# Attention probabilities of four head pairs per layer, turned by transposing DMA transfers instead of TensorE

## The chip, the cores and the metric

The kernel runs on one core of a Trainium2 chip. The metric is the device time of one execution in microseconds (us). The five engines of the core run their own instruction streams and wait for each other by semaphores: TensorE (PE; PEld is its weight load), VectorE (DVE), ScalarE (ACT), GpSimd (POOL) and SyncE (SP). SP, ACT and POOL also issue DMA transfers, each from a queue of its own (SPq, ACTq, POOLq).

## What is computed

Two decoder layers on 256 tokens of width 2048. Each layer has a mixer and a SwiGLU network. In the mixer one input projection feeds two groups of heads: eight heads of sparse attention (DSA: an indexer picks the 64 best keys of a query) and eight heads of latent attention (MLA). The part that matters here is, per head,

```
logits = einsum('bthd,bshd->bhts', q, k) * scale
p = softmax(where(mask, logits, -inf))
out = einsum('bhts,bshd->bthd', p, v)
...
mix = einsum('bse,ed->bsd', concatenate([out_a, out_b]), w_o)
```

All in float32. The sparse group is computed as a masked one, with a bias that is very negative where a key was not picked.

## The kernel before

A matrix is streamed from HBM in units of 512 KB (256 rows by 512 columns), one unit per `load_unit`. SP loads a unit into a raw buffer (line 342, a ring of four, `RAW`). ScalarE writes the high word of its values (`wh`, line 429) and VectorE the rest (`wl`, line 430), into a ring of five (`UNITS`). TensorE then runs 12 matmuls of 512 columns per unit (high by high, high by low, low by high, for two halves of the rows and two token tiles; lines 393 to 395). After each unit `tick()` advances side tasks, which are Python generators: a task that says `yield n` goes on n units later. So the code says after which unit a step is written; a scheduler then sets each engine's own order by the times that it reckons with, and a step may move past rows of other steps on that engine.

The attention of a pair of heads is such a task, `attend`. Logits of both heads go into PSUM (`att`; lines 800 and 804 for MLA, 835 for DSA), VectorE scales and masks them into tiles `lg` (one for the first 128 queries with 128 keys, one for the second with 256), ScalarE takes the exponentials, VectorE normalises. Three units later TensorE turns the probabilities, six 128 by 128 transposes per pair (`transpose4`, line 426), ScalarE copies them out of PSUM (`pr`, line 585), and a unit later TensorE multiplies by the values (lines 592 and 593) and ScalarE and VectorE split the result into `oA` or `oB`.

A layer has four MLA pairs (M0 to M3) and four DSA pairs (D0 to D3), and the units around them belong to other projections. From about 200 us on (layer 0) they come in this order: key block KA1 (8 units), query block QA1 (8 units), value block VA1 (8 units), then w_o. D0 and D1 run beside KA1, M2 and M3 beside QA1, D2 and D3 beside VA1.

One side task already turns tiles by DMA: `heads_T` (for QA0, KA1 and QA1) evacuates a projection to `hd`, ScalarE copies its 32-bit words apart into a plane of low and one of high halfwords (`pl`, line 630), its own queue issues a transposing transfer (line 633), and ScalarE interleaves the halves again (`qk`, line 639). The hidden layer does the same from SP's queue (lines 1068, 1074 and 1079). Tiles `lg`, `pl`, `pr`, `hd` and the work tiles of the rotation (`ra`, `rb`) share two rings of four and six buffers (`t2`), so a new one waits for the last reader of the old.

In the background GpSimd loads, stores and VectorE adds "pre-sums" (`presums`, tiles `q`, lines 853 to 873) for the network behind, paced by the splits.

Of the kernel before, what the change touches and what calls it, by code (L numbers as in the profile page):

```python
# [27 lines left out]
U16 = mybir.dt.uint16  # L28
AF = mybir.ActivationFunctionType
# [4 lines left out]
P = 128  # L34
D = 2048
S = 256
NT = S // P
# [27 lines left out]
SOON = 200  # L65
FIRSTD = 2
LAND = 5
BEHIND_D, LANDH = 2, 9
T2, T2MORE = 4, 6
ALLFROM, SETSFROM, EARLY = 3, 4, 0  # L70
# [17 lines left out]
def hybrid_trunk(ctx: ExitStack, tc: tile.TileContext, x, xt_in, pos, w_in, g_cq, g_ckv, w_uq,  # L88
                 w_ukv, w_o, ln1_g, ln1_b, ln1_T, w_gu, w_down, ln2_g, ln2_b, ln2_T, out):
    nc = tc.nc  # L90
# [7 lines left out]
    def nm(s):  # L98
        uid[0] += 1
        return f"{s}{uid[0]}"  # L100

    def t8(shape, dt, s):
        return sb.tile(shape, dt, name=nm(s), tag="a8", bufs=10)
# [13 lines left out]
    def pt(shape, dt, s, tag=None, bufs=1):  # L117
        assert phase["name"] == "att"
        return phase["pool"].tile(shape, dt, name=nm(s), tag=tag or s, bufs=bufs)
# [4 lines left out]
    def t2(shape, s, dt=F32):  # L124
        if phase["name"] == "att":
            phase["t2"] = phase.get("t2", 0) + 1
            if phase["t2"] * T2MORE % (T2 + T2MORE) < T2MORE:
                return pt(shape, dt, s, "t2", T2MORE)
        return sb.tile(shape, dt, name=nm(s), tag="t2", bufs=T2)
# [10 lines left out]
    def in_turn(s, first, n):  # L140
        turns[s] = turns.get(s, -1) + 1
        return bank(first + turns[s] % n, s)
# [4 lines left out]
    def trp():  # L147
        return in_turn("tr", 4, 2)

    def att():  # L150

        return ps.tile([P, 2, C], F32, name=nm("att"), tag="b67", bufs=1)
# [58 lines left out]
    def causal(m, t):  # L211
        return m if t else m[:, P:]
# [98 lines left out]
    def spawn(gen):  # L311
        task = [0, gen]
        tasks.append(task)
        step(task)
        return task

    def behind(*before):
        while any(b in tasks for b in before):
            yield 1
# [33 lines left out]
    latest = {}  # L353
# [70 lines left out]
    def transpose4(srcs, psum):  # L424
        for i, s in enumerate(srcs):
            nc.tensor.transpose(psum[:, i * P:(i + 1) * P], s, ident)

    def split(hi, lo, src):
        high = nc.scalar.activation(hi, src, AF.Copy)  # L429
        nc.vector.tensor_tensor(lo, src, f(hi), op=ALU.subtract)  # L430
        return high.ins
# [123 lines left out]
    def softmax_head(lg, t, n):  # L555

        mx = small([P, 1], "mx")
        nc.vector.tensor_reduce(mx, lg, axis=AX.X, op=ALU.max, negate=True)
        sm = small([P, 1], "sm")
        nc.scalar.activation(lg, lg, AF.Exp, bias=mx, accum_out=sm)  # L560
        rc = small([P, 1], "rc")
        nc.vector.reciprocal(rc, sm)
        nc.vector.tensor_scalar(lg, lg, rc, None, ALU.mult)

    def attend(logits_of, scale, bias, v_of, oh, ol, h0, wait=3):


        lgs = []
        lp = att()
        logits_of(h0, [[lp[:, j, 0:P], lp[:, j, P:3 * P]] for j in range(2)])  # L570
        for t in range(NT):
            n = P * (t + 1)
            lg = t2([P, 2, n], "lg")
            nc.vector.scalar_tensor_tensor(lg, lp[:, :, t * P:t * P + n], scale,
                                           bias[t].unsqueeze(1).to_broadcast([P, 2, n]), op0=ALU.mult, op1=ALU.add)
            for j in range(2):
                softmax_head(lg[:, j, :], t, n)
            lgs.append(lg)
        yield wait
        prs = []  # L580
        for j in range(2):
            tp = trp()
            transpose4([lgs[0][:, j, :], lgs[1][:, j, 0:P], lgs[1][:, j, P:]], tp)
            pr = t2([P, 3 * P], "pr")
            nc.scalar.activation(pr, tp[:, :3 * P], AF.Copy)
            prs.append(pr)
        yield 1
        op = trp()
        for j, pr in enumerate(prs):
            v0, v1 = v_of(h0 + j)  # L590
            ov = op[:, j * S:(j + 1) * S]
            mm(ov, v0, pr[:, 0:S], start=True, stop=False)
            mm(ov[:, P:], v1, pr[:, S:], start=False, stop=True)
        split(oh.rearrange("p j t -> p (j t)"), ol.rearrange("p j t -> p (j t)"), op)


    def layer(l, xT, norms, last):
# [10 lines left out]
        def heads_T(o, nh, hd, rot, cos, sin, dst, soon=False):  # L608
# [18 lines left out]
            for s in ss:  # L627
# [7 lines left out]
                yield 1  # L635
            yield LAND
            for t in range(NT):
# [134 lines left out]
        oT = {}  # L772
# [12 lines left out]
        def mla_attend(hp, m, wait, *before):  # L785

            yield wait
            yield from behind(*before)
            qn, kn, vb = m
            if "B" not in oT:  # L790
                oT["B"] = [t8([P, M_HEADS, S], F32R, "oB") for _ in range(2)]

            def logits(h0, dst):


                ts = [slice(t * P, (t + 1) * P) for t in range(NT)]
                for j in range(2):
                    for t in range(NT):
                        h = (h0 + j) % 4
                        mm(dst[j][t], qn[:, h, ts[t]], kn[:, h, :P * (t + 1)], start=t == 0, stop=False)  # L800
                for t in range(NT):
                    for j in range(2):
                        pr = slice(64 * j, 64 * j + 64)
                        mm(dst[j][t], qpT[pr, h0 // 2, ts[t]], kpT[pr, :P * (t + 1)], start=False, stop=t == NT - 1)

            h0 = 2 * hp
            yield from attend(logits, M_SCALE, [causal(masks["c"], t) for t in range(NT)],
                              lambda h: (vb[:, 0, (h % 4) * P:(h % 4 + 1) * P], vb[:, 1, (h % 4) * P:(h % 4 + 1) * P]),
                              oT["B"][0][:, h0:h0 + 2, :], oT["B"][1][:, h0:h0 + 2, :], h0, 3 if hp else 4)

        def dsa_qk(b, soon=False):
            dst = t4([P, 4, S], F32, "qk")
# [11 lines left out]
        def dsa_attend(hp, kaT, qaT, va, wait, *before):  # L824

            yield wait
            yield from behind(*before)
            if "A" not in oT:
                oT["A"] = [t8([P, A_HEADS, S], F32R, "oA") for _ in range(2)]

            def logits(h0, dst):
                for j in range(2):
                    for t in range(NT):
                        h = (h0 + j) % 4
                        mm(dst[j][t], qaT[:, h, t * P:(t + 1) * P], kaT[:, h, :P * (t + 1)], start=t == 0,
                           stop=t == NT - 1)

            h0 = 2 * hp
            yield from attend(logits, A_SCALE, bias,
                              lambda h: (va[:, 0, (h % 4) * P:(h % 4 + 1) * P], va[:, 1, (h % 4) * P:(h % 4 + 1) * P]),  # L840
                              oT["A"][0][:, h0:h0 + 2, :], oT["A"][1][:, h0:h0 + 2, :], h0)

        ready = {}

# [57 lines left out]
        bias = [pt([P, P * (t + 1)], F32, f"selb{t}") for t in range(NT)]  # L902
# [10 lines left out]
        if l == 0:  # L913
# [6 lines left out]
                             [sinM[:, t] for t in range(NT)], qpT, True))  # L920
        m = mla_half(0)
        b = [spawn(mla_attend(0, m, 1, p_qp)), spawn(mla_attend(1, m, 4, p_qp))]
        qa, p_qa = dsa_qk(QA0)
        va = dsa_v(VA0)
        finish(*b)
        a = [spawn(dsa_attend(i, ka, qa, va, 3 + 3 * i, p_ix, p_ka, p_qa)) for i in range(2)]
        m = mla_half(1)
        ka, p_ka = dsa_qk(KA1)
        b = [spawn(mla_attend(2 + i, m, 1 + 3 * i)) for i in range(2)]
        qa, p_qa = dsa_qk(QA1)  # L930
        va = dsa_v(VA1)
        finish(*a, *b)
        a = [spawn(dsa_attend(2 + i, ka, qa, va, 1 + 3 * i, p_ka, p_qa)) for i in range(2)]


# [424 lines left out]
```

## Time and profile before

| | us |
|---|---|
| median of 3 runs | 2131.24 |
| lowest, highest | 2130.05, 2131.3 |
| profiled execution | 2130.67 |
| its span (first to last instruction) | 2128.9 |
| TensorE busy in the span | 2114.6 |
| VectorE, ScalarE, GpSimd busy | 1855.1, 1363.7, 326.8 |

The granted TensorE clock was 0.998. In rows of groups, the number after the bar is the busy time of all, the next the mean of one in ns; in rows of instructions the three numbers are minimum, median and maximum in ns. In rows of waits stand the sum in us, how often, and the longest. In rows of the chain stand start and length in us. Rows of windows give, after the window, its length and each engine's busy time, then TensorE's granted clock, the share of time that the DMA engines were busy, and GB/s.

### The profile page before, as it was taken

How to read it: one execution, taken by the hardware profiler on the slowest of the kernel's cores; microseconds unless marked ns; L12 is line 12 of the kernel's file. 1: busy time of each engine (PE TensorE's matmuls, PEld its weight loads, DVE VectorE, ACT ScalarE, POOL GpSimd, SP SyncE). 2: the span in 40 equal slices, each digit the busy share in tenths (PEclk: the TensorE clock that was granted, in tenths of full speed). 3: DMA queues.
4: the chain of work that ended last, by engine and by line, in shares of the span. 5: the costliest groups of instructions: out<-in, count | busy, mean ns of one | idle time of the engine just before them, and what ended most of it. 6: DMA issues, size and time to landing. Idle time of an engine off the chain costs nothing.

```text
span 2128.9 us, 28292 instructions
## 1 busy us (share of the span) xinstructions
PE 2114.6 (99%) x9836; PEld 1754.3 (82%) x9836; DVE 1855.1 (87%) x2346; ACT 1363.7 (64%) x1735; POOL 326.8 (15%) x523
## 2 busy tenths in 40 slices
PE   9999999999999999999999999999999999999998
PEld 8888888888888888888888888888888888888886
DVE  7696776899999999999867976678999999999997
ACT  6556654766666667776655556457667676777773
POOL 1222220021111110110012232201111111110111
PEclk9999999999999999999999999999999999999999
DMA  8688888588889999998657888885989998999994
GB/s 312 205 298 294 309 297 312 183 229 258 242 256 278 290 295 293 279 266 265 217 178 240 302 290 293 319 287 187 249 260 252 286 276 272 296 283 292 293 304 118
DMA packets 191903, 567.11 MB, mean 266 GB/s; under 512 B 47776, under 2 KB 48080, under 8 KB 191120
## 3 DMA queue, kind: packets, MB, share of 16 engines
q1 hardware_dynamic: 127776, 403.10, 53.8%
q0 software_dynamic: 51024, 158.67, 29.1%
q10 hardware_dynamic: 12960, 3.54, 1.0%
q8 instruction: 77, 1.26, 0.2%
q14 instruction: 66, 0.54, 0.1%
HBM read 504.94 MB, written 31.46 MB: 252 GB/s over the span
## 4 chain that ended last, share of the span: by engine, by line
PE 85%; DVE 8%; issue 3%; DMA 2%; ACT 2%; SPq 0%; POOL 0%; DVEq 0%; ACTq 0%; POOLq 0%
PE acc L393 9%; PE acc L395 9%; PE acc L394 9%; PE acc L1222 7%; PE acc L1223 7%; PE acc L1221 7%; PE gu_p L1106 5%; PE gu_p L1107 5%; PE gu_p L1104 5%; DVE wl L430 4%; PE gu_c L1106 3%; PE gu_c L1107 3%; PE gu_c L1104 3%; PE att L1106 2%; PE att L1107 2%
## 5 line engine op out<-in xcount | busy, mean ns | idle before, releaser
L429 ACT ACTIVATE wh<-raw 128x1024 fp32r<-128x1024 f32 (+2 forms) x923 | 944.4, 1050 | 518.1 <-PE acc L395 125.8
L430 DVE TENSOR_TENSOR wl<-raw,wh 128x1024 fp32r<-128x1024 f32 (+2 forms) x923 | 1088.0, 1212 | 189.0 <-ACT wh L429 187.0
L393 PE MATMUL acc<-wh,xhl 128*128 128x512 f32 (+1 forms) x756 | 297.0, 394 | 0.0
L395 PE MATMUL acc<-wh,xhl 128*128 128x512 f32 (+1 forms) x756 | 292.1, 387 | 0.0
L394 PE MATMUL acc<-wl,xhl 128*128 128x512 f32 (+1 forms) x756 | 291.6, 386 | 0.0
L1222 PE MATMUL acc<-wl,hT 128*128 128x512 f32 x640 | 249.4, 390 | 0.2
L1223 PE MATMUL acc<-wh,hT 128*128 128x512 f32 x640 | 249.2, 389 | 0.0
L1221 PE MATMUL acc<-wh,hT 128*128 128x512 f32 x640 | 249.0, 391 | 0.0
L393 PEld LDWEIGHTS acc<-wh,xhl 128*128 128x128 f32 x756 | 142.0, 188 | 30.2 <-issue 3.6
L395 PEld LDWEIGHTS acc<-wh,xhl 128*128 128x128 f32 x756 | 141.9, 188 | 27.2
L394 PEld LDWEIGHTS acc<-wl,xhl 128*128 128x128 f32 x756 | 142.1, 188 | 26.5 <-DVE wl L430 1.1
L1222 PEld LDWEIGHTS acc<-wl,hT 128*128 128x128 f32 x640 | 120.2, 188 | 26.0 <-DVE wl L430 1.4
L1223 PEld LDWEIGHTS acc<-wh,hT 128*128 128x128 f32 x640 | 120.1, 188 | 24.9
L1221 PEld LDWEIGHTS acc<-wh,hT 128*128 128x128 f32 x640 | 120.1, 188 | 24.7
L1230 POOL DMA_DIRECT2D x<-d x80 | 68.2, 866 | 445.6 <-ACT d L1229 445.1
L1106 PE MATMUL gu_c<-wl,xhl 128*128 128x512 f32 x340 | 132.9, 391 | 0.6 <-DVE wl L430 0.6
L1107 PE MATMUL gu_c<-wh,xhl 128*128 128x512 f32 x340 | 132.3, 389 | 0.0
L1104 PE MATMUL gu_c<-wh,xhl 128*128 128x512 f32 x340 | 132.3, 389 | 0.0
L1106 PE MATMUL gu_p<-wl,many 128*128 128x512 f32 x240 | 93.7, 390 | 0.2
L1107 PE MATMUL gu_p<-wh,many 128*128 128x512 f32 x240 | 93.4, 389 | 0.0
L1104 PE MATMUL gu_p<-wh,many 128*128 128x512 f32 x240 | 93.2, 389 | 0.0
L349 POOL DMA_DIRECT2D sum<-in_w_up_dram x61 | 33.8, 554 | 367.0 <-DVE wl L430 355.0
(313 smaller groups left out, 3872.9 us busy)
## 6 DMA issues: line engine op xcount, KB each, us to landing
raw<-in_w_gate_dram SPq DMA_DIRECT2D x176, 512.0 KB, 5.5
raw<-in_w_down_dram SPq DMA_DIRECT2D x176, 512.0 KB, 7.2
raw<-in_w_in_dram SPq DMA_DIRECT2D x144, 512.0 KB, 5.5
sum<-in_w_up_dram POOLq DMA_DIRECT2D x122, 512.0 KB, 7.6
raw<-in_w_up_dram SPq DMA_DIRECT2D x101, 512.0 KB, 5.7
raw<-in_w_o_dram SPq DMA_DIRECT2D x64, 512.0 KB, 6.9
q<-q POOLq DMA_DIRECT2D x56, 512.0 KB, 5.0
raw<-q SPq DMA_DIRECT2D x56, 512.0 KB, 6.3
```

Source lines behind the costliest of these rows:

```text
L393: mm(o[t][:, :n], h, a, start=first, stop=False)
L394: mm(o[t][:, :n], h, b, start=False, stop=False)
L395: mm(o[t][:, :n], l, a, start=False, stop=final)
L429: high = nc.scalar.activation(hi, src, AF.Copy)
L430: nc.vector.tensor_tensor(lo, src, f(hi), op=ALU.subtract)
L1104: mm(o[name], h, a, start=name not in begun, stop=False)
L1106: mm(o[name], h, b, start=False, stop=False)
L1107: mm(o[name], l, a, start=False, stop=end)
L1221: mm(o[c][t], h, wh[:, j, :], start=begin, stop=False)
L1222: mm(o[c][t], h, wl[:, j, :], start=False, stop=False)
L1223: mm(o[c][t], lo, wh[:, j, :], start=False, stop=end)
L1230: nc.gpsimd.dma_start(xt[t][:, c * C:(c + 1) * C], d, accum_op=ALU.add)
```

## The change

The pairs M2, M3, D0 and D1 of each layer take a new path (`by_dma`). Per pair, ScalarE copies each `lg` into planes of halfwords, SP's queue issues one transposing transfer per `lg`, back into it, and ScalarE interleaves the halves into `pr` in four copies; the value products come `PLAND` = 4 units after the second transfer is written. The other four pairs stay as they were.

```diff
+PLAND = 4
...
-    def attend(logits_of, scale, bias, v_of, oh, ol, h0, wait=3):
+    def attend(logits_of, scale, bias, v_of, oh, ol, h0, wait=3, by_dma=False):
...
-        yield wait
         prs = []
-        for j in range(2):
-            tp = trp()
-            transpose4([lgs[0][:, j, :], lgs[1][:, j, 0:P], lgs[1][:, j, P:]], tp)
-            pr = t2([P, 3 * P], "pr")
-            nc.scalar.activation(pr, tp[:, :3 * P], AF.Copy)
-            prs.append(pr)
-        yield 1
+        if by_dma:
+            turned = []
+            yield 1
+            for t, lg in enumerate(lgs):
+                n = P * (t + 1)
+                h16 = t2([P, 4 * n], "pl", U16)
+                flat = lg.rearrange("p j n -> p (j n)").bitcast(U16)
+                with tc.issue_after(latest["high"]):
+                    nc.scalar.activation(h16.rearrange("p (h n) -> p h n", h=2), flat.rearrange("p (n h) -> p h n", h=2), AF.Copy)
+                yield 1
+                v = flat.rearrange("p (k t) -> p k t", t=P)
+                nc.sync.dma_start_transpose(v, h16)
+                turned.append(v.rearrange("p (h j b) t -> p h j b t", h=2, j=2))
+            yield PLAND
+            for j in range(2):
+                pr = t2([P, 3 * P], "pr")
+                for t in range(NT):
+                    d = pr[:, 0:P] if t == 0 else pr[:, P:]
+                    with tc.issue_after(latest["high"]):
+                        nc.scalar.activation(d.bitcast(U16).rearrange("p (b t h) -> p h b t", h=2, t=P),
+                                             turned[t][:, :, j], AF.Copy)
+                prs.append(pr)
+                yield 1
+        else:
...
-                              oT["B"][0][:, h0:h0 + 2, :], oT["B"][1][:, h0:h0 + 2, :], h0, 3 if hp else 4)
+                              oT["B"][0][:, h0:h0 + 2, :], oT["B"][1][:, h0:h0 + 2, :], h0, 3 if hp else 4, hp >= 2)
...
-                              oT["A"][0][:, h0:h0 + 2, :], oT["A"][1][:, h0:h0 + 2, :], h0)
+                              oT["A"][0][:, h0:h0 + 2, :], oT["A"][1][:, h0:h0 + 2, :], h0, by_dma=hp < 2)
```

In the new file all lines behind the first are one higher, and those behind `attend` 25 higher: `wh` is written on line 430, the planes on 589, SP's transposes are issued on 592, the copies back stand on 600, the value products on 617 and 618, the planes of `hd` on 655 and its transposes on 658.

How this moves instructions is seen at three places of layer 0. First TensorE at D1's and M2's place; before, the transposes of M2 (its `lg_2545` and `lg_2561`) stand behind the fourth unit of QA1 (`wh_2621`), right ahead of M3's logits:

```order
L395 MATMUL acc_2517<-wh_2621,xhl_70 128x512
L426 MATMUL tr_2641<-ident,lg_2545 128x128
L426 MATMUL tr_2641<-ident,lg_2561 128x128 x2
L426 MATMUL tr_2647<-ident,lg_2545 128x128
L426 MATMUL tr_2647<-ident,lg_2561 128x128 x2
L800 MATMUL att_2653<-kn_2080,qn_2079 128x128
```

Now M3's logits follow that unit (`wh_2626` here) directly, and M2's value products stand further down:

```order
L396 MATMUL acc_2805<-wh_2833,xhl_70 128x512
L617 MATMUL tr_2853<-pr_2782,vb_2081 128x256
L618 MATMUL tr_2853<-pr_2782,vb_2081 128x128
L617 MATMUL tr_2853<-pr_2828,vb_2081 128x256
L618 MATMUL tr_2853<-pr_2828,vb_2081 128x128
L394 MATMUL acc_2804<-wh_2865,xhl_68 128x512
```

The transposes are gone, and M2's value products have moved from behind the fifth unit of QA1 to behind the second of VA1; between M2's logits and them stand nine units, D1's value products and M3's logits.

Second, ScalarE from M2's exponentials (`lg_2545`, `lg_2561`) on, where it also turns KA1 (`hd_2497`, `hd_2506`). Before:

```order
L560 ACTIVATE lg_2561,sm_2565<-lg_2561,mx_2563 128x256
L560 ACTIVATE lg_2561,sm_2572<-lg_2561,mx_2570 128x256
L633 DMA_TRANSPOSE hd_2497<-pl_2595 128x8x128
L633 DMA_TRANSPOSE hd_2506<-pl_2616 128x8x128
L429 ACTIVATE wh_2745<-raw_2743 128x1024
L429 ACTIVATE wh_2779<-raw_2777 128x1024
L429 ACTIVATE wh_2831<-raw_2829 128x1024
L585 ACTIVATE pr_2645<-tr_2641 128x384
L585 ACTIVATE pr_2651<-tr_2647 128x384
```

Now (M2's tiles are `lg_2535` and `lg_2551`, KA1's `hd_2484` and `hd_2493`, D1's result `oA_2188`):

```order
L561 ACTIVATE lg_2551,sm_2562<-lg_2551,mx_2560 128x256
L658 DMA_TRANSPOSE hd_2484<-pl_2588 128x8x128
L589 ACTIVATE pl_2591<-lg_2535 128x512
L655 ACTIVATE pl_2618<-hd_2493 128x1024
L430 ACTIVATE oA_2188<-tr_2611 128x512
L658 DMA_TRANSPOSE hd_2493<-pl_2618 128x8x128
L589 ACTIVATE pl_2622<-lg_2551 128x1024
L430 ACTIVATE wh_2737<-raw_2735 128x1024
L430 ACTIVATE wh_2760<-raw_2758 128x1024
L430 ACTIVATE wh_2808<-raw_2806 128x1024
L664 ACTIVATE qk_2251<-hd_2484 128x2x4x128
```

Three more rows stand ahead of the splits: M2's two plane copies and the high half of D1's result. Behind these rows come M3's exponentials, a split, M3's planes, and then M2's copies back (`pr_2782`, `pr_2828`).

Third, SP's queue at the same place. Before it holds loads alone, the last of QA1 and the first of VA1:

```order
L342 DMA raw_2777<-in_w_in_dram 128x1024
L342 DMA raw_2829<-in_w_in_dram 128x1024
L342 DMA raw_2851<-in_w_in_dram 128x1024
L342 DMA raw_2876<-in_w_in_dram 128x1024
L342 DMA raw_2897<-in_w_in_dram 128x1024
L342 DMA raw_2915<-in_w_in_dram 128x1024
```

Now the transposes of M2 (`lg_2535`, `lg_2551`) and M3 (`lg_2656`, `lg_2672`) stand among them:

```order
L343 DMA raw_2806<-in_w_in_dram 128x1024
L343 DMA raw_2831<-in_w_in_dram 128x1024
L592 DMA_TRANSPOSE lg_2535<-pl_2591 128x4x128
L592 DMA_TRANSPOSE lg_2551<-pl_2622 128x8x128
L343 DMA raw_2863<-in_w_in_dram 128x1024
L343 DMA raw_2887<-in_w_in_dram 128x1024
L343 DMA raw_2908<-in_w_in_dram 128x1024
L592 DMA_TRANSPOSE lg_2656<-pl_2708 128x4x128
L343 DMA raw_2933<-in_w_in_dram 128x1024
L592 DMA_TRANSPOSE lg_2672<-pl_2733 128x8x128
```

The loads of VA1 behind a transpose wait with it for ScalarE's plane copies. By the program's list of waits, the first of M2's transposes also waits for both transfers of KA1 on ScalarE's queue (`hd_2484`, `hd_2493`).

More of the change, by code (lines that the diff above doesn't have):

```diff
@@ L578, in attend @@
             lgs.append(lg)
-        yield wait
         prs = []
-        for j in range(2):
-            tp = trp()
-            transpose4([lgs[0][:, j, :], lgs[1][:, j, 0:P], lgs[1][:, j, P:]], tp)
-            pr = t2([P, 3 * P], "pr")
-            nc.scalar.activation(pr, tp[:, :3 * P], AF.Copy)
-            prs.append(pr)
-        yield 1
+        if by_dma:
[22 more added lines that the diff above has]
+        else:
+            yield wait
+            for j in range(2):
+                tp = trp()
+                transpose4([lgs[0][:, j, :], lgs[1][:, j, 0:P], lgs[1][:, j, P:]], tp)
+                pr = t2([P, 3 * P], "pr")
+                nc.scalar.activation(pr, tp[:, :3 * P], AF.Copy)
+                prs.append(pr)
+            yield 1
         op = trp()
```

## The prediction

> **What bounds the kernel now.** I read the page first: its busy times, then the chain of waits that ended last.
>
> ```profile
> span 2128.9 us, 28292 instructions
> PE 2114.6 (99%) x9836; PEld 1754.3 (82%) x9836; DVE 1855.1 (87%) x2346; ACT 1363.7 (64%) x1735; POOL 326.8 (15%) x523
> PE 85%; DVE 8%; issue 3%; DMA 2%; ACT 2%; SPq 0%; POOL 0%; DVEq 0%; ACTq 0%; POOLq 0%
> ```
>
> TensorE is busy for 99% of the span and is 85% of the chain, so work taken off TensorE should shorten the run one for one, as long as TensorE does not then wait where the work was. The chain in order of time shows what the work is worth at the places that the change touches.
>
> ```profile
> 211.59 0.66 PE tr L426 x6
> ...
> 222.84 0.23 PE acc L395
> 223.07 0.66 PE tr L426 x6
> 223.72 0.23 PE acc L393
> ...
> 235.97 1.31 PE att L800 x8
> 237.29 0.86 PE att L804 x8
> ...
> 252.27 0.43 PE tr L592 x2
> 252.70 0.22 PE tr L593 x2
> ...
> 1318.29 0.66 PE tr L426 x6
> ```
>
> Six transposes stand on the chain with 0.66 us, and the 512-column matmul behind them starts at once and takes its usual 0.23 us. The eight groups that the change removes (first row 211.59, last 1318.29) all stand there. Logits of an MLA pair take 1.31 + 0.86 = 2.17 us, the value products of a pair 2 x (0.43 + 0.22) = 1.30 us.
>
> **Removed.** Eight pairs lose six transposes each: 8 x 0.66 = 5.3 us off the chain. That is the whole possible gain, 0.25% of the time; 0.2% (4.3 us) is about what a measurement of this kernel can tell from no change.
>
> Two copies out of PSUM (line 585) go per pair as well, on ScalarE, which is off the chain there.
>
> **Added on ScalarE.** The nearest rows are those of the block that already turns its tiles by DMA (lines 630, 633, 639) and those of the hidden layer (1074).
>
> ```profile
> L585 ACT ACTIVATE pr<-tr x32: 467/478/492, 162.0 to 1371.1; 128x384 f32<-128x384 f32 x32
> ...
> L630 ACT ACTIVATE pl<-hd x12: 1040/1053/1059, 172.3 to 1324.6; 128x1024 uint16<-128x1024 uint16 x12
> L633 ACTq DMA_TRANSPOSE hd<-pl x12: 1248/1326/2745, 173.4 to 1325.7; - x12
> L639 ACT ACTIVATE qk<-hd x12: 1352/1356/1368, 196.8 to 1345.6; 128x1024 uint16<-128x1024 uint16 x12
> ...
> DMA to landing us min/median/max: 3.0/4.5/9.4
> ...
> L1074 SPq DMA_TRANSPOSE g<-e x16: 1237/1658/3566, 541.2 to 1963.6; - x16
> ...
> DMA to landing us min/median/max: 4.2/5.5/7.1
> ```
>
> A pair copies 512 and 1024 halfwords into planes: 0.53 (half of 1.05, an estimate; between 0.4 and 1.05) + 1.05 us. Back come four copies with 2 x (256 + 512) halfwords: 1.5 x 1.36 = 2.0 us. Two copies of 0.48 go. Net about 2.7 us a pair, 10.7 us a layer. ScalarE is busy for 64% of the span, so the total fits; what matters is where it makes TensorE wait.
>
> **The tight place.** That is the pair M2, because the turning of key block KA1 or query block QA1 on ScalarE's own queue falls among its steps. By the order of the changed program, TensorE does between the end of M2's logits and M2's value products nine units, D1's value products and M3's logits. A unit is 2.72 us (the period of the splits when TensorE paces them, below: 271.97 to 274.69): 9 x 2.72 + 1.30 + 2.17 = 28.0 us.
>
> ```profile
> 240.94 1.26 ACTq L633 DMA_TRANSPOSE hd<-pl  x1
> ...
> 241.37 0.50 ACT L560 ACTIVATE lg<-lg,mx 128x256 f32<-128x256 f32 x1
> ...
> 242.25 2.30 ACTq L633 DMA_TRANSPOSE hd<-pl  x1
> ...
> 271.97 1.07 ACT L429 ACTIVATE wh<-raw 128x1024 fp32r<-128x1024 f32 x1 [1.61 <-PE acc L395]
> 274.69 1.06 ACT L429 ACTIVATE wh<-raw 128x1024 fp32r<-128x1024 f32 x1 [1.65 <-PE acc L395]
> ```
>
> ScalarE in the same stretch: M2's exponentials end 3.7 us after its logits (238.15 to 241.87). Then, row by row in the new order: planes of M2 and hd, a high half of D1, the second hd transpose and planes again, 0.53 + 1.05 + 0.6 + 1.25 + 1.05 = 4.5; three splits 3.0 and the copy back 1.4; M3's exponentials 1.9; a split 1.0; M3's planes 1.6. So it reaches M2's first copy back at 3.7 + 13.4 = 17.1 us. Behind that stand 1.0 + 1.4 (the copies), 2.0 + 0.6 + 1.0 + 0.6 (splits and the evacuation of QA1) and 1.0: M2's last probabilities are ready at 24.7 us, 3.3 us ahead of TensorE, if the transfers are there. ScalarE's next splits are queued behind these copies, and TensorE's units behind those; they had the same margin or more.
>
> The transfers: the changed program's list of waits lets SP's transpose of M2 start only when both hd transposes have landed. The second is issued at about 3.7 + 2.2 = 5.9, lands 4.5 later (median), SP issues M2's first and, 1.3 later, the second, which lands 5.5 later: 17.2 us, against 17.1 when ScalarE asks. With the slow ends, 9.4 and 7.1, it is 23.7: 6.6 late, of which 3.3 are covered, so TensorE would stall 3.3 us in each layer. The trace of before has one row of this very wait, value products behind their probabilities:
>
> ```profile
> PEld tr L592 <- ACT pr L585: 1.0, 2, 0.5
> ```
>
> It cost 0.5 us each time. Between 0 and 3.3 a layer I take that 0.5, since the medians land on the edge: 1.0 us in both layers. (Less than nothing is excluded: the removed groups did not wait.) The other three pairs have more room: D0's copies back come some 7 us ahead of its value products, D1's and M3's some 4 (the same count, with fewer rows between), so they cost nothing.
>
> **SP's queue.** A transpose that waits for ScalarE holds the weight loads queued behind it; the loads feed a ring of four raw buffers, and behind it five split ones, five units or 13.6 us.
>
> ```profile
> SPq L342 <- DVE wl L430: 219.5, 80, 14.5
> ```
>
> From 150 to 420 us SP waits 219.5 us for a raw buffer to come free, so it runs ahead of its data, and a transpose (1.24 to 3.57 us of issuing) uses time in which SP stood. A load kept back by a unit or two eats the raw ring, not the five split units: nothing, up to the stall above.
>
> **The DMA engines.**
>
> ```profile
> q10 hardware_dynamic: 12960, 3.54, 1.0%
> ...
> 210.00:230.00 20.00, 20.00 (x102) 16.96 (x102) 14.74 (x25) 10.16 (x20) 7.33 (x9) 1.00 0.89 335
> 230.00:250.00 20.00, 20.00 (x104) 16.01 (x103) 16.81 (x36) 13.04 (x21) 6.29 (x11) 1.00 0.85 261
> 250.00:270.00 20.00, 20.00 (x97) 16.79 (x97) 12.08 (x30) 13.95 (x23) 3.09 (x4) 1.00 0.82 269
> ...
> 290.00:310.00 20.00, 20.00 (x101) 16.93 (x100) 17.39 (x39) 11.29 (x26) 3.33 (x5) 1.00 0.65 247
> ```
>
> ScalarE's queue moved 3.54 MB, twelve transposes of 256 KB but for 0.4 MB of stores, in 1.0% of the span: 21.3 us of all sixteen engines. The change adds 8 x 384 KB = 3.1 MB, the same again: about 9.5 us a layer. The windows from 210 to 270 leave 0.11 + 0.15 + 0.18 of 20 us = 8.8 us free, and 290 to 310 another 7.0. It fits, though only just; what gives way are the loads of the pre-sums, which nobody awaits until later. I put it at nothing, with the stall above as the price if it does not fit. [...]
>
> **Behind the pairs, layer 0.** The w_o stage ends on transfers.
>
> ```profile
> 312.82 1.07 ACT wh L429
> 316.23 10.66 DMA raw<-in_w_o_dram
> ...
> 349.93 7.64 DMA raw<-in_w_o_dram
> ...
> 350.00:370.00 20.00, 18.97 (x84) 15.44 (x83) 14.60 (x17) 7.93 (x8) 0.00 (x0) 1.00 0.87 322
> ```
>
> From 316 to 358 the chain is loads of w_o, and TensorE then idles 1.0 us. That chain starts from a split at 312.82 that TensorE releases, so it should move ahead with TensorE's 4 x 0.66 = 2.6 us; if full DMA engines set it instead, the 2.6 us come back as a longer idle. I take nothing, and keep 2.6.
>
> **Sum.** The profiled execution took 2130.67 us (span 2128.9 and 1.8 around it), 0.6 under the median of the runs, 2131.24. 2130.67 - 5.3 + 1.0 = 2126.4 us, 0.2% under both: on the edge of what can be told.
>
> **The rivals.**
> - Late probabilities: the transposes land at the slow ends in M2. For it: the 9.4 us stood in layer 1 at 1236 us, under the same pre-sum loads; against it: 4.1 and 6.3 us at 240. Full price 2 x 3.3: 2130.67 - 5.3 + 6.6 = 2132.0, the same within 0.2%.
> - Given back at w_o: 2126.4 + 2.6 = 2129.0, the same. Against it: no such idle stands in layer 1.
> - One queue of transposes, slower: SP's wait for ScalarE's, with loads behind SP's and splits behind ScalarE's. If issue too is at its longest (2.75 for 1.25, 3.57 for 1.3), the last transfer lands at 23.7 + 1.5 + 2.3 = 27.5, 10.4 late, and TensorE stalls 7.1 a layer: 2130.67 - 5.3 + 14.2 = 2139.6. It decides from a stall of 4.8 us a layer (9.6 = 5.3 + 4.3), a landing some 8 us late. [...] No run here shows the two queues meeting, as before they are never in use together.
> - No transposes gone: excluded, the changed program has them no more.
>
> **How the numbers follow.** The forecast (stalls of up to 1.6 us in all) has 0.48; late probabilities 0.22; given back 0.13; one queue 0.15; 0.02 for anything else, on the slower side. Faster 0.48, same 0.35, slower 0.17. Low end: no stall and the fastest run's 0.6 less, 2130.05 - 5.3 = 2124.7. High end: 2133.5, past late probabilities in full (2132.0) and short of both mishaps together (2134.6).
>
> **What would show it.** 48 transposes fewer on line 426; TensorE's waits hold at most 0.5 us a time for the value products of M2; ScalarE's copies back wait for no transfer in D0 and D1; the idle at 358 stays at 1 us. TensorE waiting for probabilities by several us, or for splits after the hd transposes, would make it wrong; so would a longer idle at the end of w_o.

## The result: 1.4% slower, and the profile after

The changed kernel took 2160.29 us (median of 4 runs, 2159.2 to 2161.52), the kernel before beside it 2131.27 (4 runs, 2130.05 to 2132.69): a ratio of 1.014, 95% interval 1.0129 to 1.0152. Forecast were 2126.4, at most 2133.5. The profiled execution took 2160.22 us, 1.8 of it outside its span.

First the page of the changed kernel, the rows that stand against those of before.

```profile
span 2158.4 us, 28272 instructions
PE 2118.9 (98%) x9788; PEld 1753.9 (81%) x9788; DVE 1853.0 (86%) x2346; ACT 1382.7 (64%) x1767; POOL 326.0 (15%) x523
```

The 48 transposes are gone (9836 to 9788 instructions), and TensorE is nevertheless busy 4.3 us longer. It also idles more: 39.5 us in place of 14.3 (span less busy time). Where, the windows of 20 us show; before, these rows were at 20.00 us of TensorE and at clock 1.00.

```profile
250.00:270.00 20.00, 15.00 (x65) 11.74 (x63) 10.27 (x21) 15.04 (x23) 4.00 (x8) 1.00 0.84 221
270.00:290.00 20.00, 14.54 (x55) 11.98 (x56) 10.01 (x17) 11.44 (x16) 2.33 (x3) 0.74 0.76 203
290.00:310.00 20.00, 19.06 (x87) 15.53 (x85) 12.07 (x13) 9.79 (x10) 6.17 (x11) 1.00 1.00 384
...
1310.00:1330.00 20.00, 14.81 (x74) 11.75 (x72) 8.70 (x21) 7.81 (x17) 1.61 (x3) 0.98 0.73 165
1330.00:1350.00 20.00, 14.55 (x52) 11.36 (x52) 10.63 (x24) 11.83 (x20) 5.13 (x8) 0.84 0.99 254
1350.00:1370.00 20.00, 16.96 (x69) 13.79 (x70) 14.64 (x19) 13.69 (x18) 6.20 (x10) 0.84 0.93 297
```

TensorE idles 5.00 + 5.46 + 0.94 = 11.4 us in layer 0 and 5.19 + 5.45 + 3.04 = 13.7 in layer 1, and part of its work runs at a lower clock: 14.54 x 0.26 = 3.8 us lost in layer 0 and (14.55 + 16.96) x 0.16 = 5.0 in layer 1, an estimate from busy time and mean clock. (The busy time says much the same: it grew by 4.3 although 5.3 were taken out, 9.6 together.) The sum 11.4 + 13.7 + 8.8 less the 5.3 of the transposes is 28.6 us; the spans differ by 29.5. So nearly all of the loss lies in these 60 us of each layer, the place of M2 and M3. What TensorE waits for there, in the sum over the run (us, times, longest):

```profile
PE tr L617 <- ACT pr L600: 16.7, 2, 8.8
PE acc L394 <- ACT wh L430: 6.1, 2, 5.2
```

M2's value products wait for their probabilities twice, about 8 us each, where 0.5 was forecast; ahead of that the splits are late. Those of the pair's first head come without a wait, and the second head's stand. The timeline of ScalarE in layer 0 shows where both come from (start, length, and in brackets the idle time before and what ended it):

```profile
245.96 1.04 ACT L655 ACTIVATE pl<-hd 128x1024 uint16<-128x1024 uint16 x1
246.91 0.58 ACT L430 ACTIVATE oA<-tr 128x512 fp32r<-128x512 f32 x1
250.46 1.25 ACTq L658 DMA_TRANSPOSE hd<-pl  x1
251.75 1.06 ACT L589 ACTIVATE pl<-lg 128x1024 uint16<-128x1024 uint16 x1 [4.26 <-issue]
...
265.56 0.57 ACT L640 ACTIVATE hd<-acc 128x512 f32<-128x512 f32 x1
...
273.83 0.60 ACT L640 ACTIVATE hd<-acc 128x512 f32<-128x512 f32 x1 [4.89 <-DMA lg<-pl]
```

The second transpose of KA1's heads has its plane at 247.0, and ScalarE issues it only at 250.46. From 247.49, the end of the row `oA`, ScalarE does nothing, and M2's second plane, the splits and everything behind stand. SP's queue in the same stretch has the other half:

```profile
247.96 6.86 SPq L592 DMA_TRANSPOSE lg<-pl  x2
255.04 4.66 SPq L343 DMA_DIRECT2D raw<-in_w_in_dram  x3
260.67 1.28 SPq L592 DMA_TRANSPOSE lg<-pl  x1
...
262.68 1.29 SPq L592 DMA_TRANSPOSE lg<-pl  x1
```

M2's first transpose is issued at 247.96 and lands 2.4 us later, at 250.4, which is when ScalarE goes on. ScalarE's lands 3.0 later, at 253.5, and SP issues M2's second at 253.59. The program's list of waits says just this (a DMA name is a transfer that has to have landed):

```
ACT L658 DMA_TRANSPOSE hd_2484<-pl_2588 128x8x128 [waits Activation_49]
SP  L592 DMA_TRANSPOSE lg_2535<-pl_2591 128x4x128 [waits DMAHW5_49,DMAHW4_49,Activation_49]
ACT L658 DMA_TRANSPOSE hd_2493<-pl_2618 128x8x128 [waits DMAHW5_49,Activation_49]
SP  L592 DMA_TRANSPOSE lg_2551<-pl_2622 128x8x128 [waits DMASW0_49,DMAHW6_49,PE_49,Activation_49]
```

By these waits the four transposes go strictly in turn, ScalarE, SP, ScalarE, SP, each after the landing of the one before. I had read SP's two rows alone and taken both waits of the first for ScalarE's two transposes; ScalarE's own row, the third, has a wait that it does not have before. The trace has that wait too, once in each layer, as a semaphore instruction ahead of ScalarE's transposes; before, line 633 has none:

```profile
L658 ACTq EVENT_SEMAPHORE  x2: 17/17/17, 250.4 to 1326.5; - x2
```

While they take turns the raw loads behind SP's transposes stand too, and the DMA engines idle, in a place where they had little to spare. Windows of 4 us, first of the kernel before, then of the changed one (the last two columns are the share of time that the DMA engines were busy, and GB/s; a packet's whole time is counted where it starts, so a short window can come out above 1):

```profile
248.00:252.00 4.00, 4.00 (x23) 2.90 (x22) 3.75 (x12) 2.96 (x10) 1.97 (x5) 1.00 0.83 251
252.00:256.00 4.00, 4.00 (x22) 3.41 (x21) 2.90 (x7) 3.37 (x6) 1.51 (x2) 1.00 0.97 379
```

```profile
248.00:252.00 4.00, 4.00 (x19) 3.33 (x18) 0.21 (x1) 0.25 (x1) 0.00 (x0) 1.00 0.38 103
252.00:256.00 4.00, 2.31 (x9) 1.36 (x8) 2.21 (x2) 4.00 (x5) 1.16 (x2) 1.00 0.59 111
```

From 255 on the held loads and GpSimd's pre-sum loads go out together, and M3's transposes, issued at 260.67 and 262.68, land after 10.8 and 11.1 us. They still read their planes then, in ring slots that QA1's evacuation needs: the 4.89 us at 273.83 above (8.09 in layer 1). The copies back of M2's second head stand behind that evacuation on ScalarE, and TensorE behind them, although M2's own two transfers had landed at 250.4 and 256.7:

```profile
275.46 1.22 PE L617 MATMUL tr<-pr,vb 128*128 128x256 f32 x2 [8.77 <-ACT pr L600]
```

Last the clock, in windows of 2 us (the third column from the right):

```profile
270.00:272.00 2.00, 0.00 (x0) 0.00 (x0) 0.53 (x4) 0.00 (x0) 0.00 (x0) 0.76 1.33 276
272.00:274.00 2.00, 0.00 (x0) 0.00 (x0) 1.29 (x2) 0.17 (x1) 0.00 (x0) 0.50 0.85 265
...
280.00:282.00 2.00, 2.00 (x8) 1.57 (x7) 0.69 (x1) 1.16 (x3) 0.00 (x0) 0.68 0.44 86
282.00:284.00 2.00, 2.00 (x10) 1.62 (x9) 0.68 (x1) 2.00 (x3) 0.62 (x1) 1.00 0.24 45
```

TensorE had stopped at 266.7, and the clock fell to half at about 271.05 (from the mean of 0.76), 4.4 us later; TensorE went on at 275.46 and had the full clock again at about 281.3 (from 0.68), 5.8 us after. The clock stands at 0.50 for 10.24 us here and for 6.83 twice in layer 1, from the means of windows of 0.2 and 0.25 us.

### The profile page after: what moved, and what is told of

It is laid out like the page before. It is cut to its first block, busy times and chain, and to the rows that moved or that the text cites. A ratio compares the mean times of both kernels' runs of the same rounds, so it can differ in the third digit from the quotient of the medians.

```text
span 2158.4 us, 28272 instructions
## 1 busy us (share of the span) xinstructions
PE 2118.9 (98%) x9788; PEld 1753.9 (81%) x9788; DVE 1853.0 (86%) x2346; ACT 1382.7 (64%) x1767; POOL 326.0 (15%) x523
```

## The experiments

All are edits of the changed kernel unless it is said otherwise. The kernel before took 2129.9 to 2130.9 us (medians) beside them.

**One queue for all transposes.** The first run gives the heads' transposes to SP's queue.

```diff
-                nc.scalar.dma_start_transpose(v, h16)      # L658
+                nc.sync.dma_start_transpose(v, h16)
```

> The changed kernel, with the transposes of QA0, KA1 and QA1 issued from SP's queue too, so that no two queues transpose. Theory (queues waiting for each other start the loss): ScalarE's idle time ahead of M2's second plane copy (4.3 and 8.6 us) and TensorE's wait for splits behind it (5.2 us in layer 1) go, M2's probabilities come earlier; about 2140 us. Rival (buffers are held too long: ScalarE's and VectorE's waits for a slot whose last reader is a transpose of M3 make the loss): the 8 to 9 us waits for M2's probabilities stay, about 2153 us.

Measured: 2134.47 us (2128.78 to 2137.61, 10 runs), ratio 1.0016 (1.0007 to 1.0025). 26 of the 29 us are back. TensorE's wait for M2's probabilities, the landings of line 592, the same windows of 4 us, and the one of 20 us where something is left:

```profile
PE tr L617 <- ACT pr L600: 1.9, 1, 1.9
```

```profile
DMA to landing us min/median/max: 2.9/4.9/9.8
```

```profile
248.00:252.00 4.00, 4.00 (x19) 3.30 (x19) 4.00 (x7) 2.55 (x3) 3.17 (x6) 1.00 1.12 283
252.00:256.00 4.00, 4.00 (x20) 3.30 (x19) 2.42 (x12) 3.87 (x12) 0.00 (x0) 1.00 1.02 408
...
1310.00:1330.00 20.00, 18.14 (x75) 14.87 (x74) 14.15 (x33) 17.22 (x29) 4.54 (x8) 0.91 1.06 322
```

The DMA engines no longer stop, M2's wait is gone in layer 0, and one of 1.9 us, with a lower clock behind it, stays in layer 1 (at half rate for about 3.4 us, from the mean of 0.79 over the 8 us from 1324, after a pause of 1.9). M3's transposes land after 4.9 to 6.5 us. The time does not come to 5.3 us under the kernel before. It varies over 9 us; the profiled execution (2131.31) is one of the shorter, and what the longer ones wait for was not seen.

As a control, the same line changed in the kernel before:

> The kernel before, with the transposes of QA0, KA1 and QA1 issued from SP's queue. A control for one_queue: if the move of these transposes alone gains nothing, 2130 to 2132 us; if it gains time by itself (ScalarE no longer issues), 2128 us or less, and then one_queue's recovery is partly that.

Measured: 2130.06 us (2129.5 to 2131.87, 10 runs), ratio 0.9999 (0.999 to 1.0009). The move by itself gives nothing, so the 26 us come from the old transposes and the new ones together.

Is it then the number of queues? The other single queue, ScalarE's:

```diff
-                nc.sync.dma_start_transpose(v, h16)        # L592
+                nc.scalar.dma_start_transpose(v, h16)
```

> The probabilities' transposes (L592) issued by ScalarE into its own queue, where the heads' transposes (L658) are already; nothing else differs from the changed kernel. Theory (the loss comes from two queues that let only one transpose through at a time, so any single queue mends it): ScalarE no longer sits idle ahead of M2's second plane (4.26 and 8.55 us in the changed kernel), the plane's idle falls under 1 us, and the time is that of all transposes in SP's queue, 2134 us, in 2131 to 2138. Rival (it is SP's queue that mends it, because SP issues early and ScalarE's stream is held by each transpose it issues): ScalarE pays 1.2 us for each of 16 issues and waits at each for the transpose ahead, M2's and M3's copies come later, and the time is 2145 to 2160 us.

Measured: 2166.36 us (2162.93 to 2167.89, 4 runs), ratio 1.0165 (1.0151 to 1.0179). The theory that any single queue mends it falls; the rival named the direction, and its range was still too low. TensorE's wait, the landings of line 592, and ScalarE's timeline in layer 1:

```profile
PE tr L617 <- ACT pr L600: 22.2, 5, 7.2
```

```profile
DMA to landing us min/median/max: 2.6/9.4/18.0
```

```profile
1303.08 7.86 ACTq L592 DMA_TRANSPOSE lg<-pl  x2
1310.99 1.44 ACT L600 ACTIVATE pr<-lg 128x256 uint16<-128x256 uint16 x3 [6.99 <-issue]
```

There is one queue only, but when two transposes are issued back to back, the second's issue takes up to 6.56 us (the trace does not tell a wait inside it from the issuing), and ScalarE, which has to issue it, stands for that time (6.99 us). SP has such issues too, up to 4.24 us with all in its queue, and has nothing but loads behind them. And the probabilities now land after 9.4 us in the median in place of 4.9: they run beside SP's raw loads, where in SP's queue the loads stand behind them (that this order is the reason was not tried apart).

**Which of ScalarE's transposes.** Only KA1's, or only QA1's, in SP's queue:

```diff
-        def heads_T(o, nh, hd, rot, cos, sin, dst, soon=False):
+        def heads_T(o, nh, hd, rot, cos, sin, dst, soon=False, q=nc.scalar):
...
+                                      nc.sync if b == KA1 else nc.scalar))   # or QA1
```

> Only KA1's two head transposes of each layer go to SP's queue; KA0's and QA1's stay in ScalarE's. Theory (ScalarE stands still because its queued transpose of KA1's second half waits for SP's M2 transpose, and what follows, M2's second plane, the splits, M2's copies, is late by that): the idle of 4.26 and 8.55 us ahead of M2's second plane goes, and with it nearly all of the loss; 2132 to 2140 us. Rival (the waits for M3's landing ahead of QA1's evacuation, 4.9 and 8.1 us, have their own cause in ScalarE's queue): they stay, 2145 to 2155 us.

> Only QA1's two head transposes of each layer go to SP's queue; KA1's stay in ScalarE's. Theory (the loss starts at KA1's): ScalarE still idles 4 to 9 us ahead of M2's second plane, and the time is within 5 us of the changed kernel's 2160.3. Rival (QA1's make the loss): 2132 to 2145 us.

Measured: KA1's 2135.95 us (2132.25 to 2140.17, 8 runs), ratio 1.0028 (1.0017 to 1.0038); QA1's 2154.52 us (2151.91 to 2159.29, 4 runs), ratio 1.012 (1.0105 to 1.0136), 5.8 us under the changed kernel where at most 5 was expected. (The profiled execution with KA1's, 2132.25 us, is the shortest of its eight.) ScalarE in layer 0, first with KA1's in SP's queue, then with QA1's:

```profile
243.50 1.64 ACT L589 ACTIVATE pl<-lg 128x512 uint16<-128x512 uint16 x2
...
261.91 0.60 ACT L640 ACTIVATE hd<-acc 128x512 f32<-128x512 f32 x1 [1.76 <-DMA lg<-pl]
```

```profile
251.32 1.06 ACT L589 ACTIVATE pl<-lg 128x1024 uint16<-128x1024 uint16 x1 [4.73 <-issue]
...
273.48 0.60 ACT L640 ACTIVATE hd<-acc 128x512 f32<-128x512 f32 x1 [4.44 <-DMA lg<-pl]
```

With KA1's two transposes gone from ScalarE's queue M2's two planes follow each other at once, and the wait of QA1's evacuation shrinks too: it followed from the first. With QA1's gone both stay. So the loss starts at the two transposes of KA1, and these alone account for 24 of the 29 us.

**Two queues, without ScalarE's wait.** Written later, M2's planes come behind both of KA1's transposes, and ScalarE's wait for SP goes; SP's first transpose then waits for both of KA1's, which is what the prediction had taken the changed kernel to do. In the first run the wait is gone in both layers, in the second in layer 0 alone; TensorE's order is the same in both.

```diff
-PLAND = 4
+PLAND = 3      # the second run keeps 4
...
-            yield 1        # L583
+            yield 3        # 2 in the second run
```

> The probabilities' planes are written two units later and the value products three in place of four units behind the last (one unit later in all). Both queues stay. By this the second of KA1's transposes no longer waits for SP's first of M2 in either layer; SP's first waits for both of KA1's, as the prediction had assumed for the changed kernel. Theory (that one wait on ScalarE is the loss): no idle of ScalarE above 2 us ahead of M2's second plane in either layer, and 2128 to 2138 us. Rival (two queues beside each other slow each other whichever engine waits): SP's wait for KA1's makes M2's landings as late, and the time stays above 2148 us.

> The probabilities' planes are written one unit later, the value products still four units behind; TensorE's order is that of the run beside it. In layer 0 the second of KA1's transposes no longer waits for SP's first of M2; in layer 1 it still does. Theory (that one wait on ScalarE is the loss): layer 0 is free of the 4 us idle of ScalarE and of TensorE's stalls, layer 1 keeps an idle of 4 to 9 us ahead of M2's second plane and most of its 13 to 14 us of lost time; 2140 to 2150 us. Rival (two queues beside each other): both layers lose as before, above 2153 us, and no difference to the run beside it.

Measured: 2150.02 us (2145.18 to 2151.98, 5 runs), ratio 1.0085 (1.0071 to 1.0099), and 2155.12 us (2153.51 to 2156.85, 4 runs), ratio 1.0118 (1.0104 to 1.0132). My theory, that this one wait is the loss, falls: without it 10 us come back, not 26. The first run's waits, the issues of KA1's second transpose on ScalarE's queue and of M2's first on SP's, and the windows of 4 us:

```profile
PE tr L617 <- ACT pr L600: 9.9, 4, 6.4
...
PE att L860 <- DVE lg L575: 4.6, 1, 4.6
```

```profile
247.13 1.25 ACTq L658 DMA_TRANSPOSE hd<-pl  x1
```

```profile
250.29 1.20 SPq L592 DMA_TRANSPOSE lg<-pl  x1
```

```profile
248.00:252.00 4.00, 4.00 (x23) 2.86 (x22) 1.88 (x3) 3.52 (x5) 0.00 (x0) 1.00 0.58 141
252.00:256.00 4.00, 4.00 (x20) 3.30 (x19) 4.00 (x9) 3.80 (x9) 3.20 (x6) 1.00 0.84 197
```

ScalarE no longer stands, but SP does: its first transpose of M2 goes out at 250.29, when ScalarE's has landed, where the single queue had issued it at 245.74, 1.3 us behind KA1's second. The DMA engines are at 0.58 and 0.84 against 1.12 and 1.02, and M3's transposes again land after up to 12.3 us. Either wait, on ScalarE or on SP, lasts until the other queue's transfer has landed (2.4 us after its issue in the changed kernel, 247.96 to 250.4, and 3.2 here, 247.13 to 250.29) and holds up all that is queued behind it. The second run, with ScalarE's wait in layer 1 alone, is only 5 us slower, and its layer 0 loses time as well (TensorE idles 3.86 of the 20 us from 230 and 4.83 of those from 290); but its wait lasts a mere 1.4 us, so the two runs beside each other don't give the price of that wait. How the remaining 20 us of the first divide is not settled: the later value products also put D2's and D3's logits closer to what stands ahead of them (the 4.6 us wait of line 860).

**Buffers and loads.** Two rivals for the slow second half: the ring slots that the planes hold, and the pre-sum loads beside M3's transposes. First, planes of the probabilities in buffers of their own (the second ring two smaller, for space):

```diff
-T2, T2MORE = 4, 6
+T2, T2MORE = 4, 4
...
-                h16 = t2([P, 4 * n], "pl", U16)
+                h16 = pt([P, 4 * n], U16, f"plt{t}", bufs=2 - t)
```

> The changed kernel, with the planes of the turned pairs in buffers of their own (two and one) and four instead of six in the second shared ring. Rival (held buffers make the loss): ScalarE's evacuation of QA1 and VectorE's rotation no longer wait for a transpose of M3 (4.9 and 4.2 us in layer 0, 8.1 in layer 1), TensorE's 8 to 9 us waits for M2's probabilities go, about 2140 us. Theory (queues waiting for each other): ScalarE's idle 4.3 and 8.6 us stay and the time hardly moves, above 2152 us.

Measured: 2166.5 us (2163.83 to 2170.07, 4 runs), ratio 1.0167 (1.0154 to 1.018). ScalarE's waits for a landing ahead of QA1's evacuation are gone, the others grew:

```profile
ACT plt L589 <- issue: 14.5, 2, 10.2
...
ACT pr L600 <- DMA lg<-plt: 8.1, 4, 4.7
```

So the held slots pass the delay on in the changed kernel, but without them the stall comes all the same (the smaller ring may have cost something of its own). Then pre-sum loads eight units later, with two queues and with one. The edit holds back the fifth of a layer's seven sets, and with it the two behind: in layer 0 with two queues the fifth moves from 214 to 223 us to 236 to 255, and the sixth, which had stood beside M3's transposes from 256 to 261, to 283 to 302.

```diff
                 u = EARLY
+                if fc == 8:
+                    yield 8
```

> The changed kernel with the loads of the second set of pre-sums (L878), which stand between M2's and M3's probabilities, put eight units later; both queues of transposes kept. Theory (the loss is the two queues taking turns, the loads beside them only lengthen each transfer): M3's landing falls from 11 us to 5 or 6, QA1's evacuation no longer waits 4.9 and 8.1 us for it, but ScalarE's idle ahead of M2's second plane stays; 2145 to 2156 us. Rival (the load on the DMA engines makes the 11 us and with it most of the loss): 2132 to 2140 us. Rival (the load has no part): within 0.2% of 2160.

> All transposes in SP's queue, and the second set's pre-sum loads eight units later. Theory (what is left of the loss with one queue, 2134.5 against 2125.3 if only the 5.3 us came off, is M2's value products being late by 0 to 2 us when transfers land slowly under these loads, and half clock after): 2127 to 2131 us, no wait of M2's value products above 0.5 us. Rival (what is left lies elsewhere: the loads only move to DSA's value products or make the pre-sums late): 2133 to 2140 us.

Measured: 2176.48 us (2166.65 to 2179.34, 4 runs), ratio 1.0206 (1.0185 to 1.0227), and 2156.2 us (2153.7 to 2157.74, 4 runs), ratio 1.0117 (1.0101 to 1.0132). Both are worse than with the loads where they were, which no theory had expected. With two queues the probabilities do land sooner (median 4.0 us, at most 5.3; in the changed kernel 6.0 and 11.4), so M3's 11 us came with the loads beside them. Yet nothing is won: TensorE still waits 14.2 us for probabilities and, anew, for splits in the w_o stage. With one queue, first the w_o stage, then the probabilities:

```profile
PE acc L996 <- ACT wh L430: 7.8, 2, 3.9
PE tr L617 <- ACT pr L600: 7.7, 3, 4.3
```

The moved traffic falls on the next transposes: with two queues the heads' (line 658) land after up to 26.6 us (8.4 in the changed kernel), with one after up to 14.2 (7.1 without the edit). That DMA time as such is short here is my reading of it; another place for the loads was not tried.

**Each half alone.** DSA's pairs alone by DMA, and the MLA pairs alone:

```diff
-                              oT["B"][0][:, h0:h0 + 2, :], oT["B"][1][:, h0:h0 + 2, :], h0, 3 if hp else 4, hp >= 2)
+                              oT["B"][0][:, h0:h0 + 2, :], oT["B"][1][:, h0:h0 + 2, :], h0, 3 if hp else 4)
```

> D0 and D1 turn their probabilities by DMA, all MLA pairs by TensorE. Theory (the loss is made where SP's transposes meet those of ScalarE's queue, at M2 and M3): no stall of TensorE on probabilities, 4 x 0.66 = 2.6 us under the kernel before, 2128.6 us. Rival (the loss is made by the extra transfers and copies as such, wherever they are): half of them, so half of the 29 us, about 2145 us.

```diff
-                              oT["A"][0][:, h0:h0 + 2, :], oT["A"][1][:, h0:h0 + 2, :], h0, by_dma=hp < 2)
+                              oT["A"][0][:, h0:h0 + 2, :], oT["A"][1][:, h0:h0 + 2, :], h0)
```

> M2 and M3 by DMA, all DSA pairs by TensorE. Theory (meeting queues): the whole loss stays and D's 2.6 us of gain are gone, about 2163 us, with ScalarE idle 4 to 9 us ahead of M2's second plane copy and TensorE waiting 8 to 9 us for M2's probabilities in each layer. Rival (extra transfers as such): about 2145 us.

Measured: DSA 2144.39 us (2135.98 to 2150.35, 6 runs), ratio 1.0058 (1.0041 to 1.0075); MLA 2147.66 us (2141.67 to 2152.16, 4 runs), ratio 1.0076 (1.0059 to 1.0093). I had expected no loss from DSA's half, and all of it, about 2163 us, from MLA's. Both came out near the 2145 us of the rival, by which transfers and copies cost as such. In the MLA half ScalarE does not stand: SP's first transpose of M2 waits for both of KA1's, the order that the prediction had assumed, and 17 us are lost even so. (Of its waits one of 5.2 us, at line 790 ahead of M2 in layer 1, was not followed up.) What speaks against the rival is that half with one queue, below.

In the DSA half the longest wait is another one:

```profile
PE tr L427 <- DVE oA L431: 5.7, 2, 2.8
```

D1's value products, now late, stand right ahead of M2's transposes on TensorE, which need one of the two PSUM buffers `tr` and wait until VectorE has emptied it. If so, it must stay with one queue, and go when a unit more stands between. (In the first of the next two texts this is the rival; the theory there, that ScalarE's own queue held D1's result back, fell.)

> D0 and D1 by DMA, MLA by TensorE, all transposes in SP's queue. Theory (in dsa_only ScalarE was held by its own queue, so D1's result was split late and TensorE's transposes of M2 waited for its PSUM buffer): that wait (5.7 us) goes, about 2128 us. Rival (D1's value products now stand right ahead of M2's transposes and there are two PSUM buffers for both): the wait stays, 2138 us or more.

> DSA's first two pairs by DMA, the MLA pairs by TensorE, all transposes in SP's queue, and the value products three units behind in place of four, so that two units and not one stand between D1's value products and M2's transposes on TensorE. Theory (with four units the 3.5 us wait in each layer is for D1's value products to be evacuated from the one of two PSUM buffers that M2's transposes need): the wait of L427 for the evacuation falls to under 1 us in each layer; 2127 to 2131 us, against 2140.4 with four units. Rival (TensorE's transposes are late because the vector and scalar engines are behind, whatever stands ahead): the wait stays at 2 us or more and the time at 2137 to 2143.

Measured, with one queue: four units behind 2140.41 us (2137.27 to 2144.55, 4 runs), ratio 1.0049 (1.0036 to 1.0063); three units behind (`PLAND = 3`, two units between in place of one) 2136.58 us (2135.67 to 2139.1, 6 runs), ratio 1.003 (1.0019 to 1.0042). That wait in the one and in the other:

```profile
PE tr L427 <- DVE oA L431: 7.0, 2, 3.5
```

```profile
PE tr L427 <- DVE oA L431: 1.0, 2, 0.6
```

The wait went as said, the time came to 2136.6 and not to 2131: with three units ScalarE's copies back wait 12.0 us for landings of up to 11.8, in D0 and D1. One queue alone changes little in this half (2144.39 to 2140.41). And the MLA half with one queue:

> M2 and M3 by DMA, DSA by TensorE, all transposes in SP's queue. Theory (meeting queues): against mla_only's 2148 us most of the loss goes, 2130 to 2134 us. Rival (landing times under the pre-sum loads make the loss of this half): little changes, above 2142 us.

Measured: 2132.12 us (2128.7 to 2135.91, 10 runs), ratio 1.0007 (0.9998 to 1.0016), no difference to the kernel before that can be told, and 15.5 us under the same transfers and copies with two queues. Waits of 0.8 and 1.0 us at M2 and D3 take most of the 2.6 that its 24 transposes save.

**Later value products.** One queue, and `PLAND = 6`:

> All transposes in SP's queue, and value products two units later (PLAND 6). Theory (what one queue leaves of the loss are value products that wait for late landings): the 2.6 us of waits for probabilities in one_queue go and with them its clock loss; 2126 to 2129 us. Rival (the rest is made by transfers that keep weight loads back, or by buffers held longer): no better than one_queue, 2133 us or more.

Measured: 2138.64 us (2137.73 to 2141.71, 5 runs), ratio 1.0043 (1.0031 to 1.0056). M2's wait is gone (D1's value products wait 1.0 us), and line 860 waits 6.8 us in two pieces for VectorE: D3's logits follow closely on D2's, and there is one `att` buffer. So with one queue the value products come up to 2 us too early at four units and are in the way of the next pairs at six. None of these kernels is measurably faster than the one before.

## Why the prediction was wrong

- Removed: right as a count (48 transposes, line 427). With one queue TensorE's busy time is 2112.4 us, 2.2 under the kernel before, with half-rate work in it; no kernel has the 5.3 us in its time.
- The step that failed is the one on transfers in "the tight place". It let SP's transpose wait for both of ScalarE's and took 0 to 3.3 us of stall a layer, 0.5 as the value. In the trace ScalarE's second transpose waits for SP's first as well, ScalarE stands 4.26 and 8.55 us, and M2's value products are 8.77 and 7.89 us late. Even if the waits had been as I read them, the runs that make them so are 20 us (planes later) and 17 us (MLA half) slower than the kernel before, so the price was too low too.
- Slow landings at M2 were not the reason in layer 0: KA1's and M2's took 2.4 to 4.2 us there, where 4.5 and 5.5 stood in the sum (in layer 1 KA1's first took 8.4). M3's took 10.7 to 11.4 in both layers, and the sum had M3 "cost nothing".
- The count of ScalarE's rows in that step was too low as well. From the end of M2's logits (about 235.4 us in layer 0) the exponentials end after 9.4 us, not 3.7, because VectorE masks the logits only at 241.62; the first copy back starts after 26.1, not 17.1; the last ends after 40.0, not 24.7. TensorE comes after 30.5, where 28.0 were reckoned.
- "SP's queue" was put at nothing because SP had time to wait. It had; the DMA engines had not. The loads behind SP's transposes stood from 245 to 255, and from 248 on the engines with them (0.38 and 0.59 busy).
- "The DMA engines": it does fit, as the single queue shows (1.12 and 1.02 busy and no stall in layer 0), but then there is nothing left for a standstill, and moving the pre-sum loads, "which nobody awaits until later", cost 16 and 22 us.
- Not in the sum at all: the ring slots (QA1's evacuation, 4.89 and 8.09 us) and the clock (about 9 us, both layers together).
- Of the rivals, "one queue of transposes, slower" was nearest, with 0.15 and a price of 2139.6: loads stand behind SP's waits and splits behind ScalarE's. Its stall of 7.1 us a layer is near the 8.77 and 7.89 at M2 by luck, for it had them from long issues and landings of M2's own, and it left out the late splits (6.1 us), the clock and what came after. The trace shows the two queues waiting for each other, with each of four transposes behind the landing of the one before. "Late probabilities" looked for slow landings in M2, which took 2.4 and 3.1 us, and was too small. "Given back at w_o" did not happen: TensorE was busy for all of the 20 us from 350 that had an idle 1.0 before.
- The rate: the 9.5 us a layer are busy time shared by all sixteen engines, and no time to a landing. A single transfer of 256 KB took 3.0 us from issue to landing at best (87 GB/s) and 11.1 under load (24 GB/s). The issue, 1.2 us, is in these times, so they are no measure of the rate itself.

## What to carry to other kernels

When a change gives a second queue transfers that the program makes take turns with those of the first, read the waits that it gains on every engine that issues them, the old user's first: here one stood ahead of ScalarE's own transpose, a row that the change had left as it was. A transfer that an engine issues from its own queue holds that engine while it waits (ScalarE stood 4.26 and 8.55 us in the changed kernel, and 6.99 with all in its own queue, each with an issue of its own in it), so give it to the engine that has nothing else to do, and keep all of that kind in one queue: of the arrangements tried, that of SP alone gave 26 of the 29 us back, that of ScalarE alone none. And a gain of a quarter of a per cent on the bounding engine is smaller than what one stall of 5.2 us cost here, with about 3 more by the clock behind it (an estimate: half of the 5.6 us that TensorE was busy in a half-rate stretch of 6.83).

## What the runs showed of the hardware

- Transposes of two queues, which these programs' semaphores let go one at a time, follow each other at the landing (2.4 and 3.0 us here, up to 8.4); in one queue the second is issued 1.3 us behind the first.
- The issue of a transpose right behind another took up to 6.56 us in ScalarE's queue and, with all in SP's, 4.24 there, against 1.2 alone, and the engine stands meanwhile.
- Landing of the same transfer of 256 KB: 3.0 us with the DMA engines 0.38 to 0.59 busy, 11.1 and 11.4 with held-back loads and pre-sum loads beside it, at most 5.3 on line 592 (transfers of 128 KB among them) where the pre-sum loads had been moved eight units later.
- TensorE's clock fell to 0.50 about 4.4 us into a pause of 8.8 us and came back 5.8 us after it. It stood at 0.50 for 10.24 us there, for 6.83 twice in layer 1, and, with all transposes in SP's queue, for about 3.4 after a pause of 1.9 us.
